# A hybrid decoder layer whose output projection becomes seven block products of summed quarters

## The chip, the cores and the metric

The kernel runs on one core of one Trainium2 chip. TensorE (PE) does the matrix products, VectorE (DVE), ScalarE (ACT) and GpSimd (POOL) work on tiles of 128 partitions in SBUF, and SyncE (SP) issues the transfers between SBUF and DRAM, one after the other and in the order in which they are written. The metric is the device time of one execution in microseconds (us): 1713.98, the median of three runs (1711.02 to 1719.48).

## The reference, cut to what matters

```python
u = rms_norm(x, norm_g)                      # x: 2048 tokens x 1024
q_g, k_g, v_g, z_g, r_g, x_m, z_m = jnp.split(u @ w_in, cuts, axis=-1)
o_g = gla_chunked(...)                       # gated linear attention, 4 heads
o_g = head_rms_norm(o_g, gla_norm_g) * jax.nn.silu(z_g)
h_m = mlstm_chunked(...)                     # mLSTM, 4 heads
o_m = (head_rms_norm(h_m, mlstm_norm_g) + mlstm_skip * c_act) * jax.nn.silu(z_m)
x = x + jnp.concatenate([o_g, o_m], axis=-1) @ w_out    # 2048 x 2048 by 2048 x 1024
return rms_norm(x, final_norm_g)
```

All of it is float32. The change is in the last two lines.

## The kernel before

Every product is taken as three products of reduced-precision parts (`mm3`, L185): an operand is split into `hi` (a cast, L208) and `lo` (the rest, L209), and hi by hi, hi by lo and lo by hi are summed in PSUM.

The tokens go by four blocks of 512. First come four mLSTM blocks (to 690 us of the trace), then four GLA blocks, b = 0 to 3 (690 to about 1342), then the output stage. In each block the class `Proj` streams the weights of the input projection: a *piece* is a 256 KB `hi` and a 256 KB `lo`, and a list of jobs (`stream`) says in which order PE takes them. Each job of GLA is a pair of column tiles (Z, Q, K and V of a head). `fetch` keeps pieces loaded ahead: there are five buffers for `whi` and `wlo` each, and the load of a piece waits until PE has used the piece five before it. From the second block on they come as ready parts from DRAM (`w_dr`, L290). While PE does projections, the attention of the previous heads is put between, in an order that a planner (`Order`) writes out for PE at build time. The order of the other engines' instructions comes from the tile scheduler; each engine then works its own list strictly in order.

The *V* piece of a head has four parts of which PE takes 12 matmuls of 256 columns for each group of tokens; the other pieces are 12 or 24 matmuls of 512 columns. The mLSTM blocks also prepare the normalised input of the next block: `uspill` (L387 to L393) loads a tile, scales it, casts it to the one staging tile `uhs`, subtracts, and stores `hi` and `lo` to `u_dr`.

The output stage has 16 tiles of 128 tokens, and each tile takes 2 column halves x 16 `k` x 3 = 96 matmuls into `py`. For tokens 0 and 1 the mLSTM half is done at the end of the stream, and their products stay open in PSUM until the GLA half follows. Attention output comes from `o_dr` in DRAM (`ol`, split into `oh` and `ol`), the weights are split once (`fraw` into `fh` and `fl`). `y_out` adds x, squares on ACT, takes the power -1/2 on POOL, scales on DVE and stores to `out`.

## Time and profile before

| | us |
|---|---|
| median of three runs | 1713.98 (1711.02 to 1719.48) |
| the profiled execution, its own time | 1712.46 |
| its span in the trace | 1710.5 |
| PE busy | 1646.3 (96%) |
| DVE busy | 834.0 (49%) |
| ACT busy | 646.9 (38%) |
| POOL busy | 316.1 (18%) |

PE busy is the sum of its matmuls, which overlap: a busy PE is not PE at its peak. The profile's chain follows the work that ended last back to its releasers, and a stage by stage look is by windows, with busy time, granted clock and the share of the DMA engines. Weight loads, POOL subtractions and casts are seen as rows of engine, line and operation, with the tile that they write, "<-", and the tiles that they read.

### The profile page before, as it was taken

The page shows a single profiled execution, that of the slowest core. Times are in us where ns is not written, and L with a number is a line of the kernel's source. Part 1 is how long each engine was busy: PE and PEld are TensorE (multiplying, and loading weights), DVE is VectorE, ACT ScalarE, POOL GpSimd, SP SyncE. Part 2 cuts the span into 40 slices and gives each one's busy share as a digit, 9 for nine tenths or more (in the row PEclk, how much of TensorE's full clock was granted, in tenths as well). Part 3 has the DMA queues.
Part 4 walks back from the last instruction along what each step waited for, and adds up shares of the span by engine and source line. Part 5 has one row for each costly group of instructions (what it writes and reads, how often), then busy time and mean ns, then how long its engine had stood idle before and what let it go on. Part 6 is the DMA issues. An engine that isn't in the chain of part 4 may idle for free.

```text
span 1710.5 us, 25000 instructions
## 1 busy us (share of the span) xinstructions
PE 1646.3 (96%) x9020; PEld 1387.2 (81%) x9020; DVE 834.0 (49%) x1960; ACT 646.9 (38%) x1383; POOL 316.1 (18%) x330
## 2 busy tenths in 40 slices
PE   7989899999999999899999999999999999999997
PEld 5767778887888788789888988898898778888886
DVE  4957776785767577634443334323432542222221
ACT  4656755554555455312232233322332431111110
POOL 3334321220231034344201010110011100000000
PEclk9999999999999999999999999999999999999999
DMA  8677667647655756475945575467646552222220
GB/s 269 200 267 239 218 225 225 197 120 219 198 185 163 238 185 207 164 273 205 336 151 175 174 261 175 133 197 247 193 129 196 182 177 99 92 93 99 99 99 27
DMA packets 191588, 313.42 MB, mean 183 GB/s; under 512 B 21200, under 2 KB 54992, under 8 KB 191456
## 3 DMA queue, kind: packets, MB, share of 16 engines
q1 hardware_dynamic: 191456, 311.74, 55.5%
q8 instruction: 73, 1.20, 0.3%
q14 instruction: 59, 0.48, 0.1%
HBM read 227.65 MB, written 84.02 MB: 182 GB/s over the span
## 4 chain that ended last, share of the span: by engine, by line
PE 53%; DVE 2%; issue 2%; DMA 1%; ACT 1%; POOL 1%; SPq 0%; POOLq 0%; DVEq 0%; ACTq 0%
PE py L185 19%; PE pp L185 18%; PE pv L185 10%; PE po L185 2%; PE pu L185 1%; DVE bc L1020 1%; PE pt L195 1%; PE pa L185 1%; PE ptk L195 0%; DMA whi<-w_dr 0%; ACT L1012 0%; DMA uh<-u_dr 0%; DMA fraw<-in_w_out 0%; DMA wraw<-in_w_out 0%; ACT bc L1012 0%
## 5 line engine op out<-in xcount | busy, mean ns | idle before, releaser
L185 PE MATMUL pp<-uh,whi 128*128 128x512 f32 x1008 | 420.3, 417 | 12.0 <-ACT whi L208 6.0
L185 PE MATMUL pp<-uh,wlo 128*128 128x512 f32 x1008 | 399.6, 396 | 0.5 <-POOL wlo L209 0.5
L185 PE MATMUL pp<-ul,whi 128*128 128x512 f32 x1008 | 399.2, 396 | 0.5 <-DVE ul L380 0.4
L185 PEld LDWEIGHTS pp<-uh,whi 128*128 128x128 f32 x1008 | 191.4, 190 | 52.4 <-ACT whi L208 7.2
L185 PEld LDWEIGHTS pp<-uh,wlo 128*128 128x128 f32 x1008 | 190.8, 189 | 48.0 <-DMA wlo<-w_dr 1.1
L185 PEld LDWEIGHTS pp<-ul,whi 128*128 128x128 f32 x1008 | 191.2, 190 | 39.9 <-issue 4.8
L209 POOL TENSOR_TENSOR wlo<-wraw,whi 128x512 fp32r<-128x512 f32 (+1 forms) x97 | 133.3, 1381 | 156.5 <-ACT whi L208 59.9
L185 PE MATMUL pv<-whi,uh 128*128 128x256 f32 (+1 forms) x512 | 150.3, 294 | 8.0 <-DVE zs L528 8.0
L185 PE MATMUL pv<-whi,ul 128*128 128x256 f32 (+1 forms) x512 | 147.5, 288 | 0.0
L185 PE MATMUL pv<-wlo,uh 128*128 128x256 f32 (+1 forms) x512 | 147.1, 287 | 0.0
L209 DVE TENSOR_TENSOR ol<-ol,oh 128x1024 fp32r<-128x1024 f32 x30 | 36.6, 1222 | 186.1 <-ACT oh L208 186.1
L208 ACT CAST oh<-ol 128x1024 fp32r<-128x1024 f32 x30 | 31.5, 1050 | 209.8 <-DMA ol<-o_dr 209.8
L185 PEld LDWEIGHTS pv<-whi,uh 128*128 128x128 f32 x512 | 99.2, 194 | 9.8 <-DVE zs L528 8.9
L209 POOL TENSOR_TENSOR qx<-qp,qx 128x256 fp32r<-128x256 f32 x60 | 55.1, 922 | 269.9 <-ACT qx L208 269.9
L185 PE MATMUL py<-fh,oh 128*128 128x512 f32 x256 | 100.8, 394 | 0.6 <-ACT fh L208 0.6
L185 PE MATMUL py<-fl,oh 128*128 128x512 f32 x256 | 100.5, 392 | 0.2 <-DVE fl L209 0.2
L185 PE MATMUL py<-fh,ol 128*128 128x512 f32 x256 | 100.6, 393 | 0.0
L185 PEld LDWEIGHTS pv<-whi,ul 128*128 128x128 f32 x512 | 99.2, 194 | 0.7
L185 PEld LDWEIGHTS pv<-wlo,uh 128*128 128x128 f32 x512 | 99.1, 194 | 0.0
L587 DVE SCALAR_TENSOR_TENSOR c<-xm,cw,c 128x512 f32<-128x512 f32 x96 | 77.7, 816 | 14.2 <-ACT c L585 13.4
L215 POOL TENSOR_TENSOR frs<-rsa,nhalf 128x1 f32<-128x1 f32 x16 | 8.7, 543 | 339.2 <-DVE rsa L214 339.2
L840 ACT ACTIVATE C<-Tm,ga 128x516 fp32r<-128x516 f32 x60 | 43.5, 725 | 59.8 <-PE pmo L185 54.0
...
## 6 DMA issues: line engine op xcount, KB each, us to landing
whi<-w_dr SPq DMA_DIRECT2D x212, 256.0 KB, 3.2
wlo<-w_dr SPq DMA_DIRECT2D x212, 256.0 KB, 3.6
wraw<-in_w_fm SPq DMA_DIRECT2D x80, 256.0 KB, 4.1
w_dr<-whi SPq DMA_DIRECT2D x76, 256.0 KB, 3.4
w_dr<-wlo SPq DMA_DIRECT2D x76, 256.0 KB, 3.4
o_dr<-ost SPq DMA_DIRECT2D x64, 256.0 KB, 3.3
...
uh<-u_dr SPq DMA_DIRECT2D x56, 256.0 KB, 4.1
```

The lines of the kernel that those rows point to most:

```text
L185: nc.tensor.matmul(o, l, r, start=start, stop=stop, **k)
L195: nc.tensor.transpose(o, i, ident)
L208: nc.scalar.copy(hi, raw)
L209: (nc.gpsimd if "l" in pool else nc.vector).tensor_tensor(lo, raw, hi.bitcast(F32), op=ALU.subtract)
L215: nc.gpsimd.tensor_tensor(dst, a, nhalf.broadcast_to(list(src.shape)), op=ALU.pow)
L587: nc.vector.scalar_tensor_tensor(ca, xt[:, 1 + j:1 + j + TB], cw[:, t, j:j + 1], ca, op0=ALU.mult, op1=ALU.add)
L840: nc.scalar.activation(Ch, T, AF.Copy, scale=ga[:, c, h:h + 1])
L1020: nc.vector.tensor_tensor_scan(w3[:, c], ones, w3[:, c], 0.0, op0=ALU.mult, op1=ALU.add)
```

## The change

The output projection is done by two token tiles at a time (a pair) as a product of 2x2 blocks: operand and weights are cut into quarters, sums and differences of quarters are formed, and seven products of those replace eight. The pair of tiles and a half of the inner dimension (mLSTM, g = 1, or GLA, g = 0) make a *unit*.

- *Weight sums* (`combine`): during GLA block 1 (g = 0) and block 2 (g = 1) four combines each are put at four jobs (`QAT`). I call them c0 to c3 and c4 to c7. A combine loads four 256 KB parts of `w_out` into the new ring, forms four differences on POOL, and *keeps* seven of the results (g = 0) or four (g = 1): a cast to `ring[6]`, a difference in place, and two stores to `q_dr`. There are 28 + 16 = 44 keeps, with 88 stores, and 32 loads. In g = 0 the last difference is written over a tile that was kept, q11.
- *Operands*: `a_raw` loads four quarters from `o_dr`, `a_prep` gives seven steps (splits with one to two differences on POOL) that are done between the products of the units before.
- *Units*: 15, each 7 x 4 x 3 = 84 matmuls, in three PSUM tiles X, Y, Z, and seven DVE adds into `ys`. For g = 1 the sums are stored to `p_dr` (a new DRAM tensor) and read again by the GLA units. Tokens 0 and 1's mLSTM half stays as it was, with its result stored to `p_dr` by `part`.
- *Weight sets*: each of the seven weight sums is a set of 8 tiles of 256 KB. Sets 4, 5, 6 and 3 of g = 1 and sets 0 and 4 of g = 0 are loaded from `q_dr` at the start of the stage, the rest of g = 0 at the switch from g = 1 to g = 0.

```diff
+        def combine(self, g, i):
+            q = {}
+            for r in range(2):
+                for j in range(2):
+                    q[r, j] = ring[2 * r + j]
+                    d = nc.sync.dma_start(q[r, j], w_out[KT * g + 4 * r + i, :, TB * j:TB * j + TB])
+                    after([self.last, d])
+            def keep(n, v):
+                hi = ring[6].bitcast(F32R)
+                nc.scalar.copy(hi, v)
+                nc.gpsimd.tensor_tensor(v.bitcast(F32R), v, hi.bitcast(F32), op=ALU.subtract)
+                nc.sync.dma_start(q_dr[g, n, i, 0], hi.bitcast(F32))
+                nc.sync.dma_start(q_dr[g, n, i, 1], v)
+            t1, t2 = ring[4], ring[5]
+            sub(t1, q[0, 1], q[0, 0])
+            sub(t2, q[1, 1], t1)
+            sub(q[0, 1], q[1, 1], q[0, 1])
+            if g == 0:
+                keep(0, q[0, 0])
+                keep(2, q[1, 1])
+            sub(q[1, 1], q[1, 0], t2)
+            if g == 0:
+                keep(1, q[1, 0])
+            for n, v in ((3, q[1, 1]), (4, t1), (5, t2), (6, q[0, 1])):
+                keep(n, v)
...
+                    if not new and b in (1, 2) and gi in QAT:
+                        n = 4 * (b - 1) + QAT.index(gi)
+                        self.combine(n // 4, n % 4)
...
+    def unit(a, w, ys, steps, done):
+        X, Y, Z = (ps_y.tile([P, TB], F32, name="py") for _ in range(3))
+        for n, b, to, last in ((0, X, (0, 0), 0), (4, Y, (1, 1), 0), (5, X, (0, 1), 0), (1, Z, (0, 0), 1),
+                               (6, X, (1, 1), 1), (2, Y, (0, 1), 1), (3, X, (1, 0), 1)):
+            for k in range(HK):
...
+                mm(b, lh, rh, k == 0 and n in (0, 4, 1), False, **go)
+                mm(b, lh, rl, False, False, **go)
+                mm(b, ll, rh, False, k == HK - 1, **go)
+            nc.vector.tensor_tensor(ys[to], b, ys[to], op=ALU.add)
...
+            if steps:
+                steps.pop(0)()
...
+    todo = [(1, p) for p in range(1, NP)] + [(0, p) for p in (NP - 1, *range(NP - 1))]
```

On SP the loads of head 1's V pieces in GLA block 1 stood as follows before (four pieces; a row with a PE wait waits for its buffer):

```order
L290 DMA whi<-w_dr 128x512 [waits DMAHW4_49,PE_49]
L290 DMA wlo<-w_dr 128x512 [waits DMAHW5_49,PE_49]
L290 DMA whi<-w_dr 128x512 [waits DMAHW6_49,PE_49]
L290 DMA wlo<-w_dr 128x512 [waits DMAHW7_49,PE_49]
L290 DMA whi<-w_dr 128x512 [waits DMAHW0_49,PE_49]
```

In the changed kernel the same place on SP has the ring loads of c0 and the stores of its keeps between the same pieces (L322 a load of `w_out`, L329 the hi store, L330 the lo store; ring_97 is the staging slot, ring_94 q11):

```order
L322 DMA ring_94<-in_w_out 128x512 [waits DMAHW5_49]
L329 DMA q_dr<-ring_97 128x512 [waits DMAHW6_49,Activation_49]
L295 DMA whi<-w_dr 128x512 [waits DMAHW7_49,PE_49]
L330 DMA q_dr<-ring_91 128x512 [waits DMAHW0_49,Pool_49]
L295 DMA wlo<-w_dr 128x512 [waits DMAHW1_49,PE_49]
L295 DMA whi<-w_dr 128x512 [waits DMAHW2_49,PE_49]
L329 DMA q_dr<-ring_97 128x512 [waits DMAHW3_49,Activation_49]
L330 DMA q_dr<-ring_94 128x512 [waits DMAHW4_49,Pool_49]
L295 DMA wlo<-w_dr 128x512 [waits DMAHW5_49,PE_49]
L295 DMA whi<-w_dr 128x512 [waits DMAHW6_49,PE_49]
L295 DMA wlo<-w_dr 128x512 [waits DMAHW7_49,PE_49]
L329 DMA q_dr<-ring_97 128x512 [waits DMAHW0_49,Activation_49]
```

The loads of the second to fourth V piece moved behind stores that wait for ACT and POOL; one more lo store and then the fourth piece follow.

On ACT in GLA block 2, about c5, the changed kernel has casts to the staging slot (L327) between A (the scores), the transposed K, the scaled Q (`qs`) and the scaled state (`Sx`), which before stood behind one another (L730, L1049, L208, L1067):

```order
L327 CAST ring_97<-ring_94 128x512 [waits DMAHW7_49,Activation_49,Pool_49]
L327 CAST ring_97<-ring_95 128x512 [waits DMAHW1_49,Pool_49]
L785 CAST A<-pa 128x512 [waits PE_49]
L1104 CAST ktk<-ptk 128x512 [waits PE_49]
L327 CAST ring_97<-ring_96 128x512 [waits DMAHW5_49,Pool_49]
L213 CAST qs<-qt 128x512 [waits DVE_49]
L327 CAST ring_97<-ring_92 128x512 [waits DMAHW1_49,Pool_49]
L1122 ACTIVATE Sx<-Tg_8522,eb 128x256 [waits DVE_49]
```

Each of these casts waits for the store of the cast before it (a DMA wait), and the rows after it on ACT wait with it.

At the start of the output stage SP now has, behind the sums of tokens 0 and 1, the loads of set 4 (f_15175 and on):

```order
L569 DMA p_dr<-yh 128x512 [waits DMAHW7_49,DVE_49]
L1284 DMA ul_15262<-q_dr 128x512 [waits DMAHW0_49]
L1292 DMA yf_15167<-in_x 128x512 [waits DMAHW1_49,Activation_49]
L569 DMA p_dr<-yh 128x512 [waits DMAHW2_49,DVE_49]
L1292 DMA yf_15168<-in_x 128x512 [waits DMAHW3_49]
L1292 DMA yf_15169<-in_x 128x512 [waits DMAHW4_49]
L1292 DMA yf_15170<-in_x 128x512 [waits DMAHW5_49]
L1284 DMA f_15175<-q_dr 128x512 [waits DMAHW6_49]
L1284 DMA f_15176<-q_dr 128x512 [waits DMAHW7_49]
```

The set's loads stand behind two stores that wait for DVE's adds of the last product before the units.

## Rows read from the trace of the kernel before

**Rows 1.** The page's part 1, busy time of the engines with its share of the span and the instructions, and part 4, the shares of the chain that ended last by engine.

```profile
PE 1646.3 (96%) x9020; PEld 1387.2 (81%) x9020; DVE 834.0 (49%) x1960; ACT 646.9 (38%) x1383; POOL 316.1 (18%) x330
...
PE 53%; DVE 2%; issue 2%; DMA 1%; ACT 1%; POOL 1%; SPq 0%; POOLq 0%; DVEq 0%; ACTq 0%
```

**Rows 2.** Windows by stage: the window and its length, busy time (and instructions) of PE, weight loads, DVE, ACT and POOL, the granted clock of PE, the DMA engines' share, GB/s. They are GLA block 1 and the output stage.

```profile
851.00:1017.00 166.00, 164.25 (x1001) 146.35 (x1000) 57.06 (x134) 49.63 (x116) 15.15 (x16) 0.99 0.59 191
...
1372.00:1700.00 328.00, 327.78 (x1416) 265.72 (x1415) 83.80 (x129) 55.59 (x97) 8.14 (x15) 1.00 0.28 96
```

**Rows 3.** The chain in order of time, its last long part: start, length, engine, tile and line, instructions.

```profile
1372.46 307.85 PE py L185 x1329
```

**Rows 4.** Waits of PE between 851 and 1342 us: engine, what waits, its releaser; total, times and longest in us.

```profile
PE pv L185 <- DVE zs L528: 5.3, 3, 1.8
PE pt L195 <- DVE A L731: 1.3, 1, 1.3
PE py L185 <- DVE zs L528: 0.6, 1, 0.6
```

**Rows 5.** The staging tile `uhs` of the mLSTM blocks: what is done with it (ns least, median, most), what ended idle time before its instructions, and the landing of its store.

```profile
L208 ACT CAST uhs<-xk x32: 609/621/631, 76.9 to 601.7; 128x512 fp32r<-128x512 f32 x32
...
  DMA u_dr<-uhs: 7.9, 8
...
DMA to landing us min/median/max: 2.0/3.1/4.7
```

**Rows 6.** The page's part 6: transfers with their count, KB each and median us from issue to landing.

```profile
whi<-w_dr SPq DMA_DIRECT2D x212, 256.0 KB, 3.2
wlo<-w_dr SPq DMA_DIRECT2D x212, 256.0 KB, 3.6
...
u_dr<-uhs SPq DMA_DIRECT2D x32, 256.0 KB, 3.1
u_dr<-xk SPq DMA_DIRECT2D x32, 256.0 KB, 3.4
```

**Rows 7.** Timeline of SP in GLA block 1: start, length, line, transfer. The rows are whi of the first and the fourth V piece of head 1, and whi of the last V piece of head 3.

```profile
869.91 0.38 SPq L290 DMA_DIRECT2D whi<-w_dr  x1
...
878.06 0.32 SPq L290 DMA_DIRECT2D whi<-w_dr  x1
...
961.77 0.32 SPq L290 DMA_DIRECT2D whi<-w_dr  x1
```

**Rows 8.** Timeline of PE: the first matmul of the first and of the fourth V piece of head 1, the stall after the first group of tokens (idle before, and its releaser, in brackets) and the last of the 17 slow matmuls after it; last, the first matmul of the last V piece of head 3.

```profile
880.89 0.28 PE L185 MATMUL pv<-whi,uh 128*128 128x256 f32 x1
...
883.01 0.28 PE L185 MATMUL pv<-whi,uh 128*128 128x256 f32 x1
...
885.63 0.39 PE L185 MATMUL pv<-whi,uh 128*128 128x256 f32 x1 [1.75 <-DVE zs L528]
...
889.19 0.35 PE L185 MATMUL pv<-wlo,uh 128*128 128x256 f32 x1
...
966.74 0.28 PE L185 MATMUL pv<-whi,uh 128*128 128x256 f32 x1
```

**Rows 9.** Timeline of ACT in GLA block 1: the table load and the logarithm of the gates.

```profile
877.21 1.28 ACT L1012 ACT_TABLE_LOAD   x1
878.51 2.01 ACT L1012 ACTIVATE bc<-bc 128x1024 f32<-128x1024 f32 x2
```

**Rows 10.** POOL's groups from 690 to 1372 us and, last, its power in the output stage: shapes and count, busy us and mean ns of one, idle before.

```profile
L209 POOL TENSOR_TENSOR qs<-qt,qs 128x512 fp32r<-128x512 f32 x14 | 18.2, 1301 | 135.2 <-ACT qs L208 135.2
...
L215 POOL TENSOR_TENSOR frs<-rsa,nhalf 128x1 f32<-128x1 f32 x16 | 8.7, 543 | 339.2 <-DVE rsa L214 339.2
```

**Rows 11.** Timeline of ACT in GLA block 2: the scaled Q and the scaled state.

```profile
1081.83 0.62 ACT L208 CAST qs<-qt 128x512 fp32r<-128x512 f32 x1 [1.47 <-DVE qt L952]
1084.52 0.51 ACT L1067 ACTIVATE Sx<-Tg,eb 128x256 fp32r<-128x256 f32 x1 [2.06 <-DVE Tg L1082]
```

**Rows 12.** Waits of PE in the mLSTM blocks (20 to 690 us) that the splits of weights and inputs end: total, times, longest.

```profile
PE pp L185 <- POOL wlo L209: 0.5, 1, 0.5
...
PE pp L185 <- DVE ul L380: 0.2, 1, 0.2
```

**Rows 13.** Timeline of PE: the first matmul of the output stage's main part.

```profile
1365.37 0.39 PE L185 MATMUL py<-fh,oh 128*128 128x512 f32 x1
```

**Rows 14.** A window near the start in which the DMA engines are all busy (columns as in rows 2).

```profile
10.00:20.00 10.00, 8.89 (x28) 6.48 (x29) 9.37 (x25) 5.18 (x9) 3.37 (x3) 1.00 1.01 373
```

**Rows 15.** Groups of DVE and ACT in the output stage (columns as in rows 10), and PE's last matmul.

```profile
L1208 DVE SCALAR_TENSOR_TENSOR fx<-fx,frs,fg 128x512 f32<-128x512 f32 x30 | 21.2, 749 | 11.1 <-POOL frs L215 11.1
L1201 DVE TENSOR_TENSOR fx<-py,fx 128x512 f32<-128x512 f32 x30 | 19.5, 685 | 18.4 <-PE py L185 18.3
L209 DVE TENSOR_TENSOR fl<-fraw,fh 128x512 fp32r<-128x512 f32 x12 | 8.2, 692 | 6.8 <-ACT fh L208 6.8
...
L1202 ACT ACTIVATE fjk<-fx 128x512 bf16<-128x512 f32 x30 | 18.9, 632 | 47.1 <-DVE fx L1201 46.7
...
1699.99 0.39 PE L185 MATMUL py<-wr,ol 128*128 128x512 f32 x1
```

**Rows 16.** Timeline of the mLSTM stage: the subtraction of `uspill` on DVE and the selection on POOL beside it.

```profile
270.79 1.59 DVE L209 TENSOR_TENSOR xk<-xk,uhs 128x512 fp32r<-128x512 f32 x1 [1.11 <-ACT uhs L208]
...
270.66 1.17 POOL L732 TENSOR_SCALAR_AFFINE_SELECT A<-A 128x1024 fp32r<-128x1024 f32 x1
```

More of the change, by code (lines that the diff above doesn't have):

```diff
@@ L163, in fast_path @@
     o_dr = dram.tile([S // P, P, 2 * KT, P], F32, name="o_dr")
+    q_dr = dram.tile([2, 7, KT // 2, 2, P, TB], F32, name="q_dr")
+    p_dr = dram.tile([S // P, P, D], F32, name="p_dr")
     w_dr = dram.tile([2 * 32 + 4 * H, 2, P, 544], F32, name="w_dr")
@@ L243, in __init__ @@
             self.wo = [(k, j) for k in range(KT, 2 * KT) for j in range(2)]
-            self.pieces += [(("wo",) + self.wo[i] + (None,), None) for i in (2, 3, 12, 13, 14, 15)[:self.AHEAD + 1]]
+            self.pieces += [(("wo",) + self.wo[i] + (None,), None) for i in (3, 2, 12, 14, 13)]
             self.got = self.sent = 0
@@ L289, in fetch @@
                     for j, t in enumerate((hi, lo)):
-                        nc.sync.dma_start(t.bitcast(F32), w_dr[i, j, :, :n])
+                        self.last = nc.sync.dma_start(t.bitcast(F32), w_dr[i, j, :, :n])
                 else:
@@ L535, in fast_path @@
     gq = mk(ctx, "gq", 1)
+    op = mk(ctx, "op", 1)
+    ring = [op.tile([P, TB], F32, name=f"ring{i}") for i in range(7)]
     left = ctx.enter_context(ExitStack())
@@ L1226, in fast_path @@
-    for t in range(2):
-        y_out(t, py2[t], xts[t])
-    for t in range(2, S // P):
-        for i in range(2):
-            o_half(t, i)
-        xt = x_load(t)
-        py = ps_y.tile([P, 2, TB], F32, name="py")
-        for j in range(2):
-            for k in range(2 * KT):
-                y_mm(py[:, j], t, k, j, k == 0, k == 2 * KT - 1)
-        y_out(t, [py[:, 0], py[:, 1]], xt)
+    ps_y = mk(nx, "ps_y", 4, space=PSUM, reuse_waits="tile")
+    f_slot = lambda i: fw.tile([P, TB], F32R, name=f"f{i}")
@@ new lines, in fast_path, with w_set, y_load @@
+    u_pair = lambda k: [pj.up.tile([P, TB], F32R, name=f"u{c}{k}") for c in "hl"]
+    w_pair = lambda: [pj.wp.tile([P, 544], F32R, name=c, bufs=pj.AHEAD + 1)[:, :TB] for c in ("whi", "wlo")]
+    for i in range(8 * 5):
+        f_slot(i)
+    def w_set(g, n, tiles):
+        for i, t in enumerate(tiles):
+            nc.sync.dma_start(t.bitcast(F32), q_dr[g, n, i // 2, i % 2])
+        return [(tiles[2 * k], tiles[2 * k + 1]) for k in range(HK)]
+    def y_load(p, src):
+        ys = {}
+        for r in range(2):
+            for j in range(2):
+                ys[r, j] = yh[(4 * turn[0] + 2 * r + j) % 8]
+                nc.sync.dma_start(ys[r, j], src[2 * p + r][:, TB * j:TB * j + TB])
+        turn[0] += 1
+        return ys
@@ new lines, in y_out, with done @@
+    def y_out(p, ys):
+        ss = [fp.tile([P, 3], F32, name="fss", bufs=4) for r in range(2)]
+        have = set()
+        def done(r, j):
+            jk = fp.tile([P, TB], BF16, name="fjk", bufs=1)
+            nc.scalar.activation(jk, ys[r, j], AF.Square, accum_out=ss[r][:, j:j + 1])
+            have.add((r, j))
+            if (r, 1 - j) not in have:
+                return
+            nc.vector.tensor_tensor(ss[r][:, 2:3], ss[r][:, 0:1], ss[r][:, 1:2], op=ALU.add)
+            rs = fp.tile([P, 1], F32, name="frs")
+            rsqrt(rs, ss[r][:, 2:3], D, fp)
+            for i in (1 - j, j):
+                nc.vector.scalar_tensor_tensor(ys[r, i], ys[r, i], rs, fg[i], op0=ALU.mult, op1=ALU.mult)
+                nc.sync.dma_start(out[(2 * p + r) * P:(2 * p + r + 1) * P, TB * i:TB * i + TB], ys[r, i])
+        return done
@@ new lines, in p_out, with done @@
+    def p_out(p, ys):
+        def done(r, j):
+            nc.sync.dma_start(p_dr[2 * p + r][:, TB * j:TB * j + TB], ys[r, j])
+        return done
+    turn = [0]
+    yh[0:0] = [fp.tile([P, TB], F32, name=f"yf{i}", bufs=1) for i in range(4)]
+    ys = y_load(1, x)
+    NP = S // P // 2
+    wm = {n: [wo[KT + HK * r + k, j] for k in range(HK)] for n, r, j in ((0, 0, 0), (1, 1, 0), (2, 1, 1))}
+    place = {4: [0, 1, 2, 3, 4, 5, 6, 8], 5: range(9, 17), 6: range(17, 25), 3: [7, *range(25, 32)]}
@@ new lines, in fast_path @@
+    for n in (4, 5, 6, 3):
+        wm[n] = w_set(1, n, [f_slot(i) for i in place[n]])
+    wg_ = {0: w_set(0, 0, [f_slot(i) for i in range(32, 40)])}
+    wg_[4] = w_set(0, 4, [pj.slot("uhs", 1), pj.slot("xtok", 1), *w_pair(), *u_pair(1), *u_pair(3)])
+    todo = [(1, p) for p in range(1, NP)] + [(0, p) for p in (NP - 1, *range(NP - 1))]
+    a = lead[0][0]
+    nxt = a_raw(*todo[1])
+    for i, (g, p) in enumerate(todo):
+        if i + 1 < len(todo):
+            an, steps = a_prep(nxt)
+            kept = todo[i + 1][1] == p
+            yn = ys if kept else y_load(todo[i + 1][1], x if todo[i + 1][0] else p_dr)
+        unit(a, wm if g else wg_, ys, steps, (lambda r, j: None) if g and kept else (p_out if g else y_out)(p, ys))
+        if i + 2 < len(todo):
+            nxt = a_raw(*todo[i + 2])
+        a, ys = an, yn
+        if g and kept:
+            wg_[5] = w_set(0, 5, [*(pj.slot("xk", 2) for _ in range(2)), *w_pair(), *u_pair(0), *u_pair(2)])
+            wg_[1] = w_set(0, 1, [f_slot(i) for i in place[4]])
+            wg_[6] = w_set(0, 6, [f_slot(i) for i in place[5]])
+            wg_[2] = w_set(0, 2, [*u_pair(4), *u_pair(6), *w_pair(), *w_pair()])
+            wg_[3] = w_set(0, 3, [f_slot(i) for i in place[6]])
+            fg = [pj.up.tile([P, TB], F32, name="fg", tag=f"u{c}5") for c in "hl"]
+            for j in range(2):
+                nc.sync.dma_start(fg[j], fin_g[TB * j:TB * j + TB].partition_broadcast(P))
+                nc.vector.tensor_scalar(fg[j], fg[j], D ** 0.5, None, op0=ALU.mult)
```

119 lines of the change are left out of this document (62 added, 57 removed).

## The prediction

> **What bounds the kernel now.** I read the page's busy shares and the engine line of its chain first: TensorE (PE) is busy 1646.3 of 1710.5 us, and over half of the chain that ended last runs through it [rows 1]. Then the windows by stage: GLA block 1 keeps PE busy 99% of its time and the output stage all of it, while DMA stands at 0.59 in the one and at 0.28 in the other [rows 2]. The chain is almost without a gap in the output stage: 1329 matmuls in 307.85 us, 0.2316 us each [rows 3]. So there is nothing to win but matmuls, and every wait that the change brings PE is paid in full. In GLA blocks 1 to 3 PE now waits only some 7 us in all, none of them for a weight load [rows 4].
>
> **The gain.** A unit has 7 products x 4 k x 3 matmuls = 84, 15 units and the 96 for tokens 0 and 1 (their mLSTM half) make 1356 matmuls. Before, 16 token tiles x 2 halves x 16 k x 3 = 1536. 180 fewer x 0.2316 us [rows 3] = 41.7 us. The rest of PE's program keeps its order.
>
> **The combines in GLA block 1 (four of them, c0 to c3, 28 keeps).** One keep is a cast on ACT into the one staging slot, a subtraction on POOL, and two stores. The next cast has to wait until the hi store has landed, since there is one slot. The mLSTM blocks have the same pattern, one staging slot and a store of it: cast 0.62 us, and landing of the store 2.0 / 3.1 / 4.7 us (least, median, most), with 7.9 us of ACT waiting for it over 8 casts [rows 5]. A keep's cycle is then 0.62 + about 0.4 of issue + 3.1 to 3.4 [rows 5, 6] = about 4.2 us, and seven of them last 29 us. What stands behind a keep's store on SP is weight loads: SP works in order, so a load behind a store waits for that keep's cast and subtraction.
>
> Take c0. Before, the four V pieces of head 1 were issued from 869.91 (the first) to 878.06 (the fourth) [rows 7] and first used from 880.89 to 883.01, 0.7 us apart [rows 8], so the fourth has 5 us and a landing of 3.2 to 3.6 us [rows 6]: little to spare. Now four ring loads and three keeps stand ahead of the last of them. The ring loads land near 872.5, hi 0 is stored at about 874; hi 1 can be cast at 877.4 and is delayed by a logarithm's table load and activation on ACT (877.2 to 880.5, [rows 9]), lo 1 is stored near 881.3; the product that overwrites q11 waits for that to land (884.7) and takes 1.3 us on POOL [rows 10], lo 2 comes 1.3 us after it. The fourth V load goes out at about 887 instead of 878 and lands at 890.5. Before, PE waited there anyway (1.75 us, until 885.63 [rows 8]); it would now go on at about 891: 5 to 6 us late. c3 is the other kind: whi of the last V piece, issued at 961.77 for a use at 966.74 [rows 7, 8], now stands behind four ring loads and hi 0. Ring loads 961.1 to 962.9, landing 3.4, cast 0.62, store: whi goes at 966, wlo behind lo 0 (two POOL operations of 1.3 after the landing) at 968, landing 971.5 for a use at 967: 4.5 us. By the same walk c1 (the lo piece of K1's second half behind lo 2) and c2 (the lo piece of V2's third behind lo 1) cost 3.5 each, since a piece of 512 columns lasts longer than one of V. Sum 17 us.
>
> A wait costs more than itself: after the 1.75 us stall the matmuls of 256 columns stand 0.21 us apart instead of 0.12 until 889.2 [rows 8], half of TensorE's full clock (1.2 for 2.4 GHz), 17 x 0.093 = 1.6 us. Eight combines, of which I let half pay that after waits of such a length: 5 to 6 us.
>
> **The combines in block 2 (c4 to c7, 16 keeps).** Here four keeps, and what is late is ACT. For c5 two casts stand between A and the state scaling Sx. Before, qs was cast at 1081.83 and Sx scaled at 1084.52 [rows 11]. A cast that waits for the slot until about 1082.8 and the next one 4.3 us after it (1087.1) make Sx 1087.7, 3.2 us late, and PE's next output product waits for Sx. c4 costs next to nothing, c6 and c7 some 1 to 2 each: 6 us. GLA together: 17 + 6 + 5 = 28 us.
>
> Bounds for GLA: below, all slack absorbs it as in the mLSTM stage, where 64 stores of this kind [rows 6] stood among the weight loads and the splits of weights and inputs cost PE 0.5 and 0.2 us in all [rows 12]; with the late V pieces alone that is about 10 us. Above, each keep takes the longest landing of 4.7 instead of 3.4, so that every walk above grows by 1.3 x 3 keeps: 28 + 4 x 4 = 44 us. I take 28, the walk at the medians.
>
> **The first units.** Set 4 is needed by the second product, 12 matmuls x 0.2316 = 2.8 us after PE begins its first unit. Before, PE ran into this stage at 1365.37 without a stall worth naming [rows 13]. Now SP's in-order queue holds the store of the partial sum of tokens 1 ahead of set 4, and it waits for DVE until about 1366.4, then four other transfers follow: set 4 issues from 1367.8, 0.45 us each. 256 KB take 0.70 us at the 373 GB/s that a window with the DMA engines all busy shows [rows 14], so 32 loads take 22.4 us, the last lands at about 1391, and the last product still takes 2.8: 1393.6 where 84 x 0.2316 = 19.5 would have ended it at 1384.9. I take 9 us (6 to 12; the lower end if half of the loads run ahead of PE's need).
>
> **Switch to GLA's weights.** 43 transfers of 256 KB in 30 us from the switch, needed up to 36 us after it: 1 us (0 to 2). The stage's tail (last unit's add, square, scaling, store) is as before, some 10 us from PE's last matmul at 1700 to the end of the span [rows 15]: 0 to 1, put at nothing.
>
> **Output units in steady state: 0.** A GLA unit lasts 19.5 us on PE; DVE needs 7 adds x 0.685 + 7 x 0.692 + 4 x 0.749 + some 0.6 = 13.2 us, ACT 7 x 0.62 + 4 x 0.82 = 7.6, POOL 4 x 1.3 + 2 x 0.54 = 6.3 [rows 10, 15]. The quarter loads run two units ahead. Cover gone is a rival below.
>
> **Sum.** -41.7 + 28 + 9 + 1 = -3.7 us. Against the profiled execution's 1712.46 that is 1708.8. This execution lies 1.5 us under the median of the runs (1713.98), so on the median's scale I forecast 1710.
>
> The stores land in 3.1 to 3.4 us in the median [rows 5, 6]. The Trainium skill's page "DMA: Bandwidth & Descriptors" (section "Anatomy of one DMA") gives a fixed 2.0 us plus bytes over 436 GB/s, an estimate of 2.6 us for 256 KB; by it a keep would be 0.5 to 0.8 us shorter and GLA's loss some 19 us instead of 28, 1701 in all. The trace has transfers at 2.0 and at 4.7, and a median above that estimate, so the sum goes by the rows.
>
> **Rivals.**
> - Faster, 1696. The keeps run at the short end: a store lands in 2.0 us [rows 5], so a cycle is 3.0 instead of 4.2, c0 is 2 us late instead of 6 (1.2 x 3 less), c1, c2 and c5 drop out, the clock is lost twice. GLA costs about 14: -41.7 + 14 + 9 + 1 = -18, 1696 on the median's scale. For it: 64 such stores cost nothing in the mLSTM blocks [rows 12]. Against it: V pieces last 0.7 us there and 5 buffers are then only 3.5 us of work.
> - Slower, 1726. SP and ACT, both in order, are blocked at every keep by a store that lands late (4.7), since the stores now stand among the loads of a stage that moves 191 GB/s already [rows 2]. GLA costs 44: -41.7 + 44 + 9 + 1 = +12. It decides as soon as GLA and the start together cost more than 50 us (from a keep's cycle of about 5.2 us).
> - Slower, 1730: DVE and POOL exclude each other in the output units. In the mLSTM stage the subtraction of two operands in SBUF took 1.59 us instead of 0.69 while POOL's selection ran beside it [rows 16]. The Trainium skill's page "SBUF — State Buffer" (section "Who interferes with whom") says that a DVE instruction with two SBUF inputs and a GpSimd instruction that reads SBUF exclude each other for the whole instruction; that row agrees. If they add up, DVE 13.2 and POOL 6.3 fill a unit's 19.5 us and each unit slips 1 to 2 us: 15 units, +20. Against it: the DVE adds read PSUM and only one tile of SBUF, and these are 4.8 of the 13.2.
> - That the change leaves out fewer matmuls than said can be excluded: the count is in the program.
>
> **How the numbers follow.** A measurement of this kernel can't tell less than about 0.5% (8.6 us: under 1705.4 or over 1722.6) from no change. My forecast (GLA 20 to 36, 1702 to 1718) has 0.42, the faster rival 0.32, the slower one of the landing 0.17, that of the ports 0.09. Of the first, 0.08 falls under 1705.4, the rest within 0.5%; of the slower rivals 0.01 is left within. Faster 0.40, same 0.35, slower 0.25. Range for 8 in 10: 1689 (GLA 10, start 6: -24.7) to 1727 (GLA 44, switch 2); the forecast's own 1702 to 1718.
>
> **What would show it.** The changed profile should show PE waiting in block 1 for whi and wlo loads, longest at the last V piece of heads 1 and 3, 3 to 6 us each; in block 2 PE waiting on the scaled state, and casts that idle before "DMA q_dr<-ring" on ACT; the window of the first unit with 9 us of PE idle, waiting for set loads; steady units at 19.5 us per unit without a gap; the py matmuls 180 fewer at 0.23. Wrong if GLA's windows last as long as before (then 1680 to 1690), or if units last over 20.5 us (then the ports or POOL bound them).

## The result and the profile after

The changed kernel takes 1734.01 us, the median of four runs (1730.47 to 1739.03), against 1713.98 before: a ratio of 1.0115 with an interval of 1.0079 to 1.0152. It is slower by 20 us, where 1710 was forecast and 1689 to 1727 given as the range. The profiled execution, the slowest of the four, has a span of 1737.3 us, 26.8 more than before.

The page's part 1 of the changed kernel (as in [rows 1]):

```profile
PE 1627.3 (94%) x8840; PEld 1364.8 (79%) x8840; DVE 937.0 (54%) x2097; ACT 693.4 (40%) x1486; POOL 496.3 (29%) x466
```

PE has 180 matmuls fewer, as counted, and is idle for 46 us more. POOL works 180 us more. The windows of GLA blocks 1 and 2 (columns as in [rows 2]) show where PE fell behind:

```profile
851.00:1017.00 166.00, 145.03 (x846) 127.66 (x846) 53.97 (x115) 56.86 (x122) 68.67 (x57) 0.92 0.76 252
1017.00:1183.00 166.00, 153.25 (x896) 134.65 (x895) 57.21 (x124) 51.25 (x116) 50.05 (x43) 0.97 0.72 246
```

Before, 164.25 of 166 us were busy at a granted clock of 0.99, POOL was busy 15 us, and the DMA engines stood at 0.59 [rows 2]. Now the clock is 0.92 in block 1, POOL has 69 us, DMA 0.76. PE's waits between 851 and 1342 us, the longest groups (columns as in [rows 4]):

```profile
PE pv L190 <- DMA wlo<-w_dr: 12.2, 7, 4.1
PE pv L190 <- DMA whi<-w_dr: 7.5, 4, 3.6
PE pv L190 <- DVE zs L581: 6.4, 2, 4.7
PE pp L190 <- DMA wlo<-w_dr: 4.2, 4, 1.8
PE po L190 <- POOL A L787: 3.1, 1, 3.1
```

All of them together are 35.5 us instead of 7.2, and two thirds are weight loads, of which there was none. As a mark for what follows I take PE's first matmul of the output projection (`py` from t_xk and t_R): at 1339.31 us before, at 1384.53 now, 45.2 us later. PE's matmuls up to the mark are the same, in the same order, in both kernels, so that each can be followed. The one that starts at 690.00 us before, where GLA begins, starts at 692.49 now, so 2.5 of the 45.2 us are older than GLA. GLA itself lost 42.7 us: block 1 takes 29.7 longer, block 2 15.5, and blocks 0 and 3 together 2.5 less. PE's timeline about c0:

```profile
885.67 0.39 PE L190 MATMUL pv<-wlo,uh 128*128 128x256 f32 x1 [2.03 <-DMA wlo<-w_dr]
886.71 0.39 PE L190 MATMUL pv<-whi,uh 128*128 128x256 f32 x1 [0.30 <-DMA whi<-w_dr]
887.99 0.58 PE L190 MATMUL pv<-wlo,uh 128*128 128x256 f32 x1 [0.77 <-DMA wlo<-w_dr]
890.62 0.58 PE L190 MATMUL pv<-whi,uh 128*128 128x256 f32 x1 [1.41 <-DMA whi<-w_dr]
891.77 0.58 PE L190 MATMUL pv<-wlo,uh 128*128 128x256 f32 x1 [0.35 <-DMA wlo<-w_dr]
```

They stand at the loads that the walk had named, but there are five of them, one close behind the other. The first matmul after a stall takes 0.39 us after the first two and 0.58 from the third on: the windows of 5 us from 885 have a granted clock of 0.72, 0.50 and 0.75 (the number behind the five busy times with their counts is the clock):

```profile
885.00:890.00 5.00, 2.46 (x10) 1.76 (x10) 5.00 (x11) 2.34 (x4) 2.30 (x2) 0.72 0.83 267
890.00:895.00 5.00, 4.03 (x17) 3.73 (x18) 1.57 (x7) 2.66 (x5) 1.64 (x2) 0.50 0.63 213
895.00:900.00 5.00, 5.00 (x35) 5.00 (x35) 0.42 (x1) 0.89 (x2) 2.04 (x2) 0.75 0.50 179
```

0.50 is TensorE's lower level, 1.2 GHz. Of the 29.7 us of block 1, 19.6 are waits beyond those of before, all of them for weights; the other 10 are matmuls at the lower clock.

Block 2 has 10.5 us of waits beyond those of before and 5 of slower matmuls. Its waits are others: the longest are 4.7 us for `zs` of DVE (1.8 before), 3.1 for A of POOL, 2.2 for a weight load and 1.6 for `on` of ACT. The first of them, with POOL's four differences of a combine beside five scans (cumulative sums) of DVE, which take 1.69 us in the kernel before:

```profile
1072.06 5.29 POOL L1210 TENSOR_TENSOR ring<-ring,ring 128x512 f32<-128x512 f32 x4 [17.77 <-DMA ring<-in_w_out]
1076.39 3.59 DVE L1075 TENSOR_TENSOR_SCAN bc<-ones,bc 128x128 f32<-128x128 f32 x5 [2.72 <-ACT bc L1067]
1085.32 0.58 PE L190 MATMUL pv<-whi,uh 128*128 128x256 f32 x1 [4.68 <-DVE zs L581]
```

From the first of these scans to `zs` DVE needs 8.2 us where it needed 5.3 before, and PE waits 2.9 us longer. For A, POOL stands idle until a ring load has landed, does its difference, and comes to the selection on A only then:

```profile
1133.08 1.26 POOL L1210 TENSOR_TENSOR ring<-ring,ring 128x512 f32<-128x512 f32 x1 [5.37 <-DMA ring<-in_w_out]
1134.29 1.10 POOL L787 TENSOR_SCALAR_AFFINE_SELECT A<-A 128x1024 fp32r<-128x1024 f32 x1
1135.44 0.39 PE L190 MATMUL po<-v,A 128*128 128x256 f32 x1 [3.11 <-POOL A L787]
```

In the output stage the first unit's second product waits for set 4, and the next matmuls are slow as well:

```profile
1421.72 3.56 PE L190 MATMUL py<-f,as 128*128 128x512 f32 x7 [7.98 <-DMA f<-q_dr]
1424.65 4.16 PE L190 MATMUL py<-f,as 128*128 128x512 f32 x10
```

17 matmuls take over 7 us there instead of 4, and the first unit lasts 32.6 us. The other mLSTM units take 19.35, but for the third (23.1, with a wait of 1.9 for an add of DVE). Of the GLA units the first takes 19.3, the next two 20.7 and 20.8, and the last five 20.0 to 20.3. PE ends at 1724.7, 313.9 us after its first unit's start; 335.0 less the 41.7 would have been 293.3. The end of the span is 12.6 us behind PE's last matmul instead of 10.1. The sum: -41.7 + 45 + 21 + 2.5 = +27, the difference of the spans.

### The profile page after: what moved, and what is told of

Read it like the earlier page. It is cut to its first block, busy times and chain, and to the rows that moved or that the text cites. A ratio compares the mean times of both kernels' runs of the same rounds, so it can differ in the third digit from the quotient of the medians.

```text
span 1737.3 us, 25765 instructions
## 1 busy us (share of the span) xinstructions
PE 1627.3 (94%) x8840; PEld 1364.8 (79%) x8840; DVE 937.0 (54%) x2097; ACT 693.4 (40%) x1486; POOL 496.3 (29%) x466
## 5 line engine op out<-in xcount | busy, mean ns | idle before, releaser
L190 PE MATMUL py<-f,as 128*128 128x512 f32 x720 | 178.0, 400 | 11.3 <-DMA f<-q_dr 8.5
L190 PEld LDWEIGHTS py<-f,as 128*128 128x128 f32 x720 | 136.6, 191 | 47.0 <-issue 10.2
L190 PE MATMUL pv<-wlo,uh 128*128 128x256 f32 (+1 forms) x512 | 150.7, 294 | 12.4 <-DMA wlo<-w_dr 12.2
L213 ACT CAST as<-ring 128x512 fp32r<-128x512 f32 x105 | 64.5, 620 | 202.6 <-PE py L190 177.9
L1210 POOL TENSOR_TENSOR ring<-ring,ring 128x512 f32<-128x512 f32 x77 | 102.2, 1331 | 147.0 <-issue 48.4
L190 PEld LDWEIGHTS pv<-whi,uh 128*128 128x128 f32 x512 | 101.8, 199 | 19.5 <-DVE zs L581 9.8
L214 DVE TENSOR_TENSOR as<-ring,as 128x512 fp32r<-128x512 f32 x105 | 87.4, 837 | 8.1 <-ACT as L213 6.9
L1306 DVE TENSOR_TENSOR yf<-py,yf 128x512 f32<-128x512 f32 x56 | 38.7, 690 | 73.2 <-PE py L190 66.5
L982 DVE TENSOR_TENSOR vl<-pv,v 128x256 fp32r<-128x256 f32 x56 | 23.7, 422 | 100.9 <-ACT v L980 100.9
```

Of the source, the lines that this page charges most:

```text
L190: nc.tensor.matmul(o, l, r, start=start, stop=stop, **k)
L213: nc.scalar.copy(hi, raw)
L214: (nc.gpsimd if "l" in pool else nc.vector).tensor_tensor(lo, raw, hi.bitcast(F32), op=ALU.subtract)
L982: nc.vector.tensor_tensor(vl[b, h][t // 2][:, t % 2, :], pv[:, :DV], vv[b, h][:, t, :].bitcast(F32), op=ALU.subtract)
L1210: nc.gpsimd.tensor_tensor(o, a, b, op=ALU.subtract)
L1306: nc.vector.tensor_tensor(ys[to], b, ys[to], op=ALU.add)
```

## The experiments

Ratios are to the kernel before, run on the same chip (1708.5 to 1711.3 us there, so compare ratios and not times); the changed kernel's is 1.0115. "Mark" is the start of PE's first output matmul (1339.31 before, 1384.53 changed). Since it also holds what an execution was early or late by before GLA, the table has the length of GLA from the matmul at 690.00 us before to the mark, against the kernel before, in the one profiled execution of each kernel.

| kernel | ratio | GLA longer by, us |
|---|---|---|
| the changed kernel | 1.0115 | 42.7 |
| three others with its GLA part (changes in the output stage alone) | 1.0103, 1.0082, 1.0107 | 41.0, 36.2, 42.3 |
| no weight sums | 0.9838 | -3.7 |
| stores from the engines' own queues | 1.0241 | 56.6 |
| stores left out | 1.0184 | 48.0 |
| steps spread | 1.0004 | 14.5 |
| sums on DVE | 1.0004 | 19.5 |
| both | 0.9914 | 2.1 |
| four others with that GLA part | 0.9900, 0.9861, 0.9862, 0.9919 | 5.4, 7.1, 7.1, 11.2 |

Kernels with the same GLA part lie up to 9 us apart, so a few us between two rows say nothing.

**No weight sums.** GLA's `combine` calls are taken out, and the sets read other weights.

```diff
-                    if not new and b in (1, 2) and gi in QAT:
+                    if False:
...
-            nc.sync.dma_start(t.bitcast(F32), q_dr[g, n, i // 2, i % 2])
+            nc.sync.dma_start(t.bitcast(F32), w_dr[28 * g + 4 * n + i // 2, i % 2, :, :TB])
```

> The weight sums are left out: no combine in the GLA blocks (no ring loads, no differences, no keeps, no stores), and the weight sets are read from the input projection's split weights instead, so that the units' products are those of other numbers. All else is as in the changed kernel. Theory (all of the GLA blocks' 45 us and nothing of the output stage's 21 comes from the combines): about 1734 - 45 = 1689 us, PE at its first output matmul as early as before (1339 us in the trace), first unit still 12 us late. Rival (the new pools, the smaller scratch or another order in the blocks cost part of it): 1700 to 1734.

1684.04 us, ratio 0.9838 (0.9821 to 0.9855); mark at 1336.97. The theory held. All of GLA's loss is the combines', and the output stage alone would bring 1.6%.

**Stores from the engines' own queues.**

```diff
-                nc.sync.dma_start(q_dr[g, n, i, 0], hi.bitcast(F32))
-                nc.sync.dma_start(q_dr[g, n, i, 1], v)
+                nc.scalar.dma_start(q_dr[g, n, i, 0], hi.bitcast(F32))
+                nc.gpsimd.dma_start(q_dr[g, n, i, 1], v)
```

> Same work and same bytes as the changed kernel, but each keep's hi store is issued by ACT behind its cast and its lo store by POOL behind its subtraction, none by SP. Theory A (weight loads stand behind keep stores on SP, in order): PE's waits for whi and wlo in GLA block 1 (20.8 us) go, block 1 gets 20 to 29 us shorter, about 1706 to 1714; the waits of block 2 on ACT and POOL stay. Rival B (the loads land late since the DMA engines are fuller): the waits stay, 1730 or more. Rival C (POOL and ACT time of the combines): also stays.

1751.94 us, 1.0241 (1.0220 to 1.0262), mark 1398.24: slower still. The waits for weights did mostly go, and others came. PE's longest waits in GLA:

```profile
PE pv L190 <- DVE zs L581: 13.2, 3, 6.6
PE pu L190 <- ACT ktk L1104: 10.5, 2, 7.3
PE po L190 <- POOL A L787: 7.1, 4, 3.5
PE pv L190 <- DMA whi<-w_dr: 4.1, 2, 2.5
```

So none of the three expectations fits alone. The order on SP made the waits for weights; with it gone, what the keeps do to ACT, POOL and DVE comes out. How much of it comes from ACT and POOL issuing the stores themselves was not tried apart.

**Steps spread over the jobs.** `combine` becomes a generator that stops after the ring loads and after each keep; each job of GLA blocks 1 to 3 (`SPB`) takes one step (`SPN`).

```diff
-                    if not new and b in (1, 2) and gi in QAT:
-                        n = 4 * (b - 1) + QAT.index(gi)
-                        self.combine(n // 4, n % 4)
+                    if not new and b in SPB:
+                        for _ in range(SPN(b, gi)):
+                            next(self.sums, None)
```

> Same work and same bytes, but the combines are taken apart: one step (the four ring loads, or one keep) at each of the 54 jobs of GLA blocks 1 to 3 instead of whole combines at eight jobs. Theory A (a keep's store that has to wait for its cast and the slot blocks SP): most stores find their tile ready, GLA's loss falls from 45 to 15 to 25 us, 1704 to 1714. Rival B (bytes): no change, 1730 or more.

1710.13 us, 1.0004 (0.9989 to 1.0018), mark 1354.11: GLA loses 14.5 us instead of 42.7, with the same work and bytes. The bytes go over three blocks here instead of two, but block 1 moves 244 GB/s against 252 in the changed kernel, and 250 in the run below that has hardly a loss left, so it isn't the traffic.

**The combines' stores left out.** The sets read other weights, as in the first run.

```diff
-                nc.sync.dma_start(q_dr[g, n, i, 0], hi.bitcast(F32))
-                nc.sync.dma_start(q_dr[g, n, i, 1], v)
```

> The combines stand where the changed kernel has them, with their loads, differences, casts and subtractions, but the 88 stores are left out and the weight sets are read from the input projection's split weights (the units' products are those of other numbers). A cast then waits for a subtraction but for no landing. Theory A (a store's wait for cast, subtraction and landing, in order on SP and ACT): GLA's loss falls from 45 to 0 to 8 us, 1684 to 1692. Rival C (the engine time of 44 casts and 76 POOL instructions, DVE shut out by POOL): 1705 or more.

1740.28 us, 1.0184 (1.0157 to 1.0210). This was the run that felled my theory of the stores: without a single one of them the kernel is slower. PE waits for weights for 2.6 us in all, but once for 11.4 us for `zs`, DVE's product:

```profile
882.67 2.73 DVE L1072 TENSOR_TENSOR_SCAN bc<-ones,bc 128x128 f32<-128x128 f32 x5 [7.51 <-ACT bc L1064]
892.35 0.68 DVE L578 SCALAR_TENSOR_TENSOR zs<-th,pp 128x512 f32<-128x512 f32 x1
893.08 0.58 PE L189 MATMUL pv<-whi,uh 128*128 128x256 f32 x1 [11.37 <-DVE zs L578]
```

DVE begins the scans 3 us later than in the kernel before, since ACT with its casts brings `bc` later, and needs 9.7 us from there to `zs` instead of 5.3. What lengthens DVE's part is seen in the changed kernel too. In the kernel before, five gate scans (over two operands in SBUF) and the copy behind them ran as in the first fence, in the changed kernel as in the second:

```profile
879.60 1.69 DVE L1020 TENSOR_TENSOR_SCAN bc<-ones,bc 128x128 f32<-128x128 f32 x5 [2.72 <-ACT bc L1012]
881.20 0.14 DVE L1021 COPY blast<-bc 128x4 f32<-128x4 f32 x1
```

```profile
881.59 2.36 DVE L1075 TENSOR_TENSOR_SCAN bc<-ones,bc 128x128 f32<-128x128 f32 x5 [3.64 <-ACT bc L1067]
883.88 0.14 DVE L1076 COPY blast<-bc 128x4 f32<-128x4 f32 x1
883.93 2.38 DVE L1075 TENSOR_TENSOR_SCAN bc<-ones,bc 128x128 f32<-128x128 f32 x4
886.24 1.17 DVE L1076 COPY blast<-bc 128x4 f32<-128x4 f32 x1
```

Beside them POOL subtracts, at these times:

```profile
881.11 1.30 POOL L328 TENSOR_TENSOR ring<-ring,ring 128x512 fp32r<-128x512 f32 x1
884.60 1.43 POOL L1210 TENSOR_TENSOR ring<-ring,ring 128x512 f32<-128x512 f32 x1 [2.19 <-DMA q_dr<-ring]
886.11 1.27 POOL L328 TENSOR_TENSOR ring<-ring,ring 128x512 fp32r<-128x512 f32 x1
```

Each of POOL's instructions holds a DVE instruction back by 0.7 to 1 us, even a copy of four columns. From the first scan to `zs` DVE needs 8.0 us (881.6 to 889.6) instead of 5.3 (879.6 to 884.9). In the run without stores a cast follows the last one after 2.0 us in the median (4.0 in the changed kernel), and POOL subtracts in 1.3 of every 2 to 2.4 us:

```profile
887.63 1.26 POOL L327 TENSOR_TENSOR ring<-ring,ring 128x512 fp32r<-128x512 f32 x1 [1.15 <-ACT ring L326]
889.62 1.31 POOL L327 TENSOR_TENSOR ring<-ring,ring 128x512 fp32r<-128x512 f32 x1 [0.73 <-ACT ring L326]
```

**The combines in mLSTM blocks.** Whole ones at three jobs of each of blocks 1 to 3; then one step at every job there and the rest at GLA's jobs without V or Z.

```diff
-QAT = (2, 6, 10, 14)
+QAT = (1, 4, 7)
...
-                    if not new and b in (1, 2) and gi in QAT:
-                        n = 4 * (b - 1) + QAT.index(gi)
-                        self.combine(n // 4, n % 4)
+                    if new and b in (1, 2, 3) and gi in QAT:
+                        n = 3 * (b - 1) + QAT.index(gi)
+                        if n < 8:
+                            self.combine(n // 4, n % 4)
```

> The same whole combines, one slot and the same queue, but at jobs 1, 4 and 7 of mLSTM blocks 1 to 3 instead of GLA blocks 1 and 2. Theory A (a burst of keeps is dear where V pieces of 0.7 us leave a weight load only some 4 us of room; in the mLSTM blocks a piece is 2.8 us of PE's work): GLA's loss of 45 us goes and the mLSTM blocks lose 0 to 15: 1684 to 1700. Rival D (what costs is ACT held at the cast, which hurts wherever it stands, and the mLSTM blocks have the busier ACT and DVE): 1710 or more, with PE waiting for ctk, zs and uh.

> One step of a combine per job, in mLSTM blocks 1 to 3 at every job and then at GLA's jobs that hold no V piece and no Z. Theory A: loss of 0 to 10 us in all, 1684 to 1694; the best of the placings. Rival D: 1700 or more.

1754.66 us, 1.0258 (1.0226 to 1.0289), and 1723.91 us, 1.0078 (1.0056 to 1.0100). GLA is free of its waits, but the mLSTM blocks, whose DVE is busy two thirds of the time, lose 67 and 38 us up to the matmul at 690.00: in the first run PE waits there for `C` (7.7 us, 0.6 before), `qp` (6.1, 0.8 before), `v1l` and others of DVE and ACT, and 9.5 us for weights. That a weight load has more room there did not help. Rival D's times came; of the waits that it named, that for `ctk` grew (6.8 to 8.3 us), those for `zs` and `uh` did not come. Spread from the mLSTM jobs on, the steps are not told apart from whole combines in GLA (1.0078 to 1.0115) and are slower than spread over GLA's jobs (1.0004).

**The combines' sums on DVE.**

```diff
-                nc.gpsimd.tensor_tensor(v.bitcast(F32R), v, hi.bitcast(F32), op=ALU.subtract)
+                nc.vector.tensor_tensor(v.bitcast(F32R), v, hi.bitcast(F32), op=ALU.subtract)
...
-            sub(t1, q[0, 1], q[0, 0])
+            sub(t1, q[0, 1], q[0, 0], nc.vector)
```

> The combines stand where they stood, whole, with all stores on SP, but their 32 differences and 44 subtractions of keeps run on DVE instead of POOL. Theory C (while POOL subtracts, DVE is shut out: the gate scans beside it took 2.4 us instead of 1.4, and PE waits for what DVE then brings late): GLA's loss falls from 45 to 20 to 32 us, 1709 to 1719. Theory A alone (only the order of stores and loads on SP costs): nothing changes, 1724 or more. Rival E (52 us more of work on DVE delay it as much): 1724 or more, with PE waiting for zs.

1711.01 us, 1.0004 (0.9988 to 1.0021), mark 1356.28 (this execution came to GLA 2.5 us earlier than the one before). Whole combines, same places, same queue: GLA loses 19.5 us instead of 42.7, and by the ratios the kernel is 19 us faster, by taking the sums from POOL. The waits for `A` and `on` are gone, and the five scans are at their old length, though DVE has 52 us more to do:

```profile
879.22 1.68 DVE L1075 TENSOR_TENSOR_SCAN bc<-ones,bc 128x128 f32<-128x128 f32 x5
880.81 0.14 DVE L1076 COPY blast<-bc 128x4 f32<-128x4 f32 x1
```

What is left are waits for weights, and those got shorter too (24.2 to 14.9 us), to which a keep's subtraction of 0.69 instead of 1.30 us fits. So the edit does two things, it frees DVE and POOL's list and it shortens the keep, and this run does not part them:

```profile
PE pv L190 <- DMA whi<-w_dr: 8.0, 4, 3.7
PE pv L190 <- DMA wlo<-w_dr: 5.8, 6, 2.0
PE pv L190 <- DVE zs L581: 4.4, 2, 2.6
PE pp L190 <- DMA wlo<-w_dr: 0.6, 1, 0.6
PE pp L190 <- DMA whi<-w_dr: 0.5, 1, 0.5
```

**Both: steps spread, sums on DVE.** The edits of those two runs, together.

> One step of a combine per GLA job, and the differences and subtractions on DVE: both causes eased. If A and C are the two parts of the loss: GLA's loss 0 to 12 us, 1684 to 1698, below the 1710 of the spread alone. If C plays no part: 1706 or more.

1696.24 us, 0.9914 (0.9896 to 0.9933), mark 1340.99: GLA is at 2 us of its old length (5 to 11 in the four other kernels with this GLA part), the windows of blocks 1 to 3 have a clock of 0.99 or 1.00, and PE's waits there are close to those of before (8.9 us instead of 7.2):

```profile
PE pv L191 <- DVE zs L588: 5.1, 3, 1.7
PE pv L191 <- DMA whi<-w_dr: 1.8, 3, 1.1
PE pt L201 <- DVE A L793: 1.1, 1, 1.1
```

Each of the two edits works alone, and the second still does on top of the first. By the ratios each gives back 19 us and both together 34; by the length of GLA 28, 23 and 41. Whether they overlap is within the scatter of the table.

**The start of the output stage.**

```diff
+        for n, b, to, last in (seven[i] for i in seq):
...
-    ys = y_load(1, x)
...
         wm[n] = w_set(1, n, [f_slot(i) for i in place[n]])
+        if n == 4:
+            ys = y_load(1, x)
...
+    for j in range(2):
+        nc.sync.dma_start(p_dr[1, :, TB * j:TB * j + TB], yh[6 + j])
     wg_ = {0: w_set(0, 0, [f_slot(i) for i in range(32, 40)])}
```

> Only the start of the output stage: the last partial sum of tokens 1 is stored behind the weight sets, set 4 goes ahead of the x tiles, and the first unit takes its products in the order 0, 1, 4, 5, 2, 6, 3, so that two products of weights that are there already come first. Theory (set 4's loads stand behind what waits for DVE): the wait of 8 us before the second product falls to 0 to 2 and the first unit's loss from 12 to 3 to 6; 1725 to 1728. Rival (the 32 loads' bandwidth sets the first unit's end whatever the order): the waits move to later products, 1731 to 1734.

1730.73 us, 1.0103 (1.0078 to 1.0128), not told apart from the changed kernel: what the rival expected. The wait for set 4 did fall (to 1.4 and some of 0.2), but 2.8 us for the add that lacked its x tile came in:

```profile
1412.55 0.49 PE L190 MATMUL py<-f,as 128*128 128x512 f32 x1 [1.38 <-DMA f<-q_dr]
...
1420.79 5.61 PE L190 MATMUL py<-f,as 128*128 128x512 f32 x12 [2.76 <-DVE yf L1308]
```

**One set for four.**

```diff
-        wm[n] = w_set(1, n, [f_slot(i) for i in place[n]])
+        wm[n] = w_set(1, n, [f_slot(i) for i in place[n]]) if n == 4 else wm[4]
```

> Sets 5, 6 and 3 of the mLSTM half are not loaded; set 4 stands for them (24 of the loads at the start are left out, the units' products of these sets are those of other numbers). Theory (set 4's place in the queue sets the first wait of 8 us, the bytes of the other sets only the 3 to 4 us after it): the wait of 8 us stays, the slow products after it go, 3 to 4 us faster than the changed kernel. Rival (bytes alone): the first unit's whole loss of 12 us falls to 5 or less.

1722.78 us, 1.0082 (1.0056 to 1.0108). The times alone don't tell it from the changed kernel; the trace does. The wait for set 4 is still 5.9 us, but the stage, from its first unit to its last product, lasts 303.6 us instead of 313.9 (311 to 314 in the other kernels with the same start): the waits of the third unit and of the switch are gone as well, and the first unit lasts 27.9 us instead of 32.6. More than I had expected hangs on the bytes, so both expectations are half right.

**The units' sums on DVE.** The four operand sums per unit go from POOL to DVE.

```diff
-            nc.gpsimd.tensor_tensor(raw["t"], raw[1, 0], raw[1, 1], op=ALU.add)
+            nc.vector.tensor_tensor(raw["t"], raw[1, 0], raw[1, 1], op=ALU.add)
...
-            sub(raw[1, 0], raw[0, 0], raw[1, 0])
+            sub(raw[1, 0], raw[0, 0], raw[1, 0], nc.vector)
```

> Only the operand sums of the output units (four per unit) move from POOL to DVE; the combines are as in the changed kernel. If POOL's sums shut DVE out there (splits of 1.45 us beside 0.69) and that is what makes a GLA unit 20.0 instead of 19.4 us: 3 to 6 us faster than the changed kernel, 1723 to 1726. Rival (the row scaling in order on DVE ahead of the add sets it): no change, 1727 to 1732.

1729.97 us, 1.0107 (1.0085 to 1.0128): the rival held. POOL does hold DVE back there too, splits of 0.69 us take 0.85 in the mean in the changed kernel's output stage and 0.69 with the sums on DVE, but a GLA unit stays at 20.0 us.

**All three together.** Steps spread, all sums on DVE, and the start as in the run on it.

> Steps spread over the jobs, all sums on DVE, and the start of the output stage with set 4 ahead: the candidate for a kernel faster than both. With A and C as the parts of GLA's loss and 2 to 4 us from the start: 1680 to 1695. If it is not under 1700, a third cause is left.

1694.81 us, 0.9900 (0.9879 to 0.9922), the fastest kernel that gives the full result, 1% faster than the kernel before and 2% than the changed one. Beside the run without the changes of the output stage (0.9914) it isn't told apart.

**Row scaling behind the next add.** On top of spread steps with the combines' sums on DVE; the second run has the change of the start too, and the third ends each unit with its last scaling.

```diff
-            if last:
-                done(*to)
+            if held:
+                f, o = held.pop()
+                f(*o)
+            if last:
+                held.append((done, to))
```

> The kernel with spread steps and sums of the combines on DVE (1696 us, 0.9914 of the kernel before), and one thing more: a finished row half is squared, scaled and stored only after the next product's add, so that no add stands behind row scaling on DVE. Theory F (a GLA unit lasts 20.0 instead of 19.4 us because PE's next unit waits for the add of its sixth product, which stands behind two row scalings): units of 19.4, 3 to 5 us faster than without, ratio 0.988 to 0.990. Rival (something else sets the unit): 0.991 or more.

> As e15_late_rows, and the start changed as in e4_start but with the x tiles ahead of set 4 again: tokens 1's partial sums stored behind the sets, first unit in the order 0, 1, 4, 5, 2, 6, 3. In e4_start the wait for set 4 fell from 8 to 2 us and a wait of 2.8 us on an add that lacked its x tile came in its place. If the queue's order is what is left to win at the start: 3 to 5 us faster than e15_late_rows. Rival (the bytes of the sets: without 24 of the loads the stage was 10 us shorter): 0 to 2 us.

> As e15_late_rows, but the last row half of a pair is scaled and stored before the next unit's tiles are loaded (in e15_late_rows and e17_start2 it is stored from a tile that has been loaded again, so that this quarter of the output holds other numbers). Within a unit no add stands behind a row scaling. Theory F: most of the gain stays, ratio 0.985 to 0.989. If the delay across the unit's border made the gain: 0.990 or more.

1689.91 us, 0.9861 (0.9838 to 0.9884); 1689.34 us, 0.9862 (0.9840 to 0.9884); 1696.39 us, 0.9919 (0.9900 to 0.9937). In the first, the waits of 0.3 to 0.4 us at the third product of the GLA units are gone, the last five last 19.4 to 19.6 us, and its stage is 8.5 us shorter than with row scaling at once: 4.5 in the GLA units, the rest in the first and third unit. The gain is a little more than theory F had expected. The second run met its rival. The waits end with an add that stands behind two scalings on DVE:

```profile
1648.27 1.42 DVE L1326 SCALAR_TENSOR_TENSOR yh<-yh,frs,fg 128x512 f32<-128x512 f32 x2 [0.67 <-POOL frs L220]
1649.60 0.69 DVE L1306 TENSOR_TENSOR yf<-py,yf 128x512 f32<-128x512 f32 x1
1650.43 0.94 PE L190 MATMUL py<-t_xk,as 128*128 128x512 f32 x3 [0.31 <-DVE yf L1306]
```

(The changed kernel.) In the third the waits are back, at the same places: the delay across the unit's border made the gain, as its second expectation has it. So what the unit's 0.6 us hang on is shown, and a form that stores every part from its own tile was not found. The order of the start brings nothing on top, and the run with one set for four points to the bytes.

## Why the prediction was wrong

- **The gain** held: 180 matmuls, 0.23 us each, and without the combines the kernel is 1.6% faster.
- **Where GLA stalls** held to the microsecond for c0: the fourth V load was to go out at 887 and went at 887.82. The walk along SP's order was right about PE's waits for weights in block 1 (17 us were expected, 19.6 came). Combine by combine it was rougher: c0 cost 3.1 us of waits beyond the 1.75 of before, and slower matmuls made PE 6.6 us late by it, where 5 to 6 were put; c1 cost 3.4 for 3.5, c2 6.6 for 3.5 and c3 5.9 for 4.5. That the sum came so near is luck in part.

```profile
887.82 0.38 SPq L295 DMA_DIRECT2D whi<-w_dr  x1
```

- **The step that failed** is GLA's sum of 28 us (42.7 measured, 36 to 42 in three other kernels with the same GLA part), in two of its terms. The larger is the clock: 5 to 6 us put, some 15 measured (45.2 us more in blocks 1 and 2, less 30.1 of waits). I let one stall of 1.75 us and its 1.6 us stand for half of the combines. Here five stalls follow each other within 7 us, and the clock is at half from the third of them on and until 897.
- **The other term is block 2:** 6 us were put on ACT, with PE waiting for the scaled state; 10.5 us of waits came, and none on the scaled state. POOL's work had been priced as its own 1.3 us in the keep's chain, as if DVE had the block to itself and nothing else stood on POOL's list. I had the row [rows 16] and used it for the output units alone. The runs showed `zs` late by 2.9 us since DVE's scans stood still beside POOL, A late behind a ring difference on POOL, and 19 to 23 us of gain from moving the sums to DVE. A part of that gain is the shorter keep and the weight loads behind it; in block 1 of the changed kernel weights came last in every wait of note, and DVE's lateness there shows only in the two runs that took the stores from SP. The Trainium skill's page "SBUF — State Buffer" (section "Who interferes with whom") says that a DVE instruction with two SBUF inputs contends with a GpSimd instruction that reads SBUF, calls this an exclusive lock, and says that copies can contend too; the scans of 2.36 for 1.69 us and the copy of 1.17 for 0.14 agree.
- **The landing of a store** was over-sized: 3.1 to 3.4 us were put in, the page of the profile has 2.2 for the 88 stores. The keep's cycle held all the same: 4.2 us were put, and from cast to cast within a combine it was 4.0 in the median (2.7 to 7.5), since the casts also waited for POOL and for other work on ACT. That it held is luck in part. The faster rival had the landing nearly right and the cycle of 3.0 wrong.

```profile
q_dr<-ring SPq DMA_DIRECT2D x88, 256.0 KB, 2.2
```

- **The output stage** was put at 9 + 1 us and cost 21, and 2.5 in the tail. The first unit cost 13 instead of 9: the wait came as worked out (8 us), the half clock after it had been left out. The third unit cost 4 and the units at the switch some 3, on adds of DVE. The last five GLA units cost 0.5 to 0.8 us each where nothing was put: the unit was said to be free of DVE because its work, 13 us, fits into 19.5; it is its order that counts, an add behind two scalings. Why the tail is longer was not tried.
- **The rivals.** The slower one of late landings gave 1726 and the right side by the wrong mechanism: stores landed early, not late. That of the ports had a mechanism that is at work and put it in the wrong stage: in the output units it is worth nothing measurable, in GLA it is a part of the loss.

What stays open: how the clock's 15 us divide between bursts and POOL, how much of the gain on DVE is the shorter keep and how much is DVE no longer held back, and how the 57 us that GLA lost with stores from the engines' own queues divide between ACT and POOL; none was tried apart.
